# A hybrid decoder layer on one core: the output product of the convolution's rows in Strassen's blocks

## The chip, the cores and the metric

The kernel runs on one core of a Trainium2 chip. The metric is device time in microseconds for one execution. The core has a matrix engine (TensorE, "PE" in the profile, with its weight loads shown apart as "PEld"), a vector engine (VectorE, "DVE"), a scalar engine (ScalarE, "ACT"), GpSimd ("POOL") and a sync engine ("SP") that issues most transfers. A difference of 0.2% is about 1.7 us here.

## The reference, cut to what matters

```python
D_MODEL = 2048; SEQ = 512; CONV_WIDTH = ATTN_WIDTH = 1024
h = rms_norm(x, norm_g)
z = h @ w_in                       # 2048 -> 7 x 1024
...                                # causal depthwise convolution, LayerNorm, swish
y_a = (u @ conv_pw_w + conv_pw_b) * silu(a_gate)      # 512 x 1024, "the convolution's rows"
...                                # dilated window attention, 16 heads
y_b = o.reshape(bsz, s, ATTN_WIDTH) * silu(b_gate)    # 512 x 1024
y = jnp.concatenate([y_a, y_b], axis=-1) @ w_out      # (512 x 2048) @ (2048 x 2048)
return x + y
```

All inputs and the result are float32. The change concerns the last product alone: the half of its rows of `w_out` that meets `y_a`.

## The kernel before

Every tensor is held transposed: features on the 128 partitions, the 512 tokens along the free dimension. A float32 product is made of three 16-bit ones. Each operand is scaled by a power of two (from a bound on its norm, `bound`, which costs one tiny matmul over `ones16`, a reduction on VectorE and a few small operations), rounded to a high part in float16, and the rest is kept as a low part, also float16. `tri` (L360) then adds high by high, high by low, and low by high in the same PSUM bank. ScalarE makes the high part of the weights (`split_hi`, L286), VectorE the low part (`split_lo`); every VectorE call goes through one helper and so has line L72 in the profile.

The work is a list of units. A unit is 512 input features (4 tiles of 128) by 512 output features of one weight matrix, 1 MB in float32, loaded into one of six raw buffers. It takes 4 output tiles x 4 input tiles x 3 matmuls = 48 matmuls of 512 tokens. Groups of units (`GROUPS`, L48) run in a fixed order: seven input projections, the pointwise projection of the convolution (`pw`), and then the output product as `wb`, `wa` and `wc`, each for four blocks of 512 output features. `wb` meets rows 0 to 511 of `y_b` (one unit each), `wa` the 1024 rows of `y_a` (two units each), `wc` rows 512 to 1023 of `y_b` (one unit each). So the output product is 4 + 8 + 4 units.

A unit has eight slots of 6 matmuls, and `clock` counts them. The program order on each engine is written by hand: `after(n, fn)` puts a piece of work n slots later. The engines run in order, so a piece that waits holds back what is behind it on its engine. `put_y` (L551) collects `y`: part `a` from `pw`, parts `b0` and `b1` from the attention; when a part is complete its bound is taken and `split16` makes its 16-bit parts on VectorE, every second slot. `evac` (L689) adds a finished PSUM bank to `res`, which starts as `x` (`fetch_res`) and lives in four 128x512 tiles per block of output features; `wc`'s evacuation stores the row. `last_matmuls` (L760) cuts the very last output tile into 384 and 128 tokens, so that only a small evacuation and store stand behind the last matmul.

```python
def tri(ps, a, b, first, last):
    (ah, al), (bh, bl) = a, b
    T.matmul(ps, ah, bh, start=first, stop=False)
    T.matmul(ps, ah, bl, start=False, stop=False)
    T.matmul(ps, al, bh, start=False, stop=last)
```

PSUM has eight banks: four in `lin_ps` for the products, four in `s_ps` for the attention, the bounds and small sums. Four part buffers (`part_pool`) hold the float16 parts of two units.

Of the kernel before, what the change touches and what calls it, by code (L numbers as in the profile page):

```python
# [10 lines left out]
F32 = mybir.dt.float32  # L11
R32 = mybir.dt.float32r
F16 = mybir.dt.float16
# [63 lines left out]
def layer(ctx: ExitStack, tc: tile.TileContext, xt, w1, w2, w3, g_in, conv_w, conv_b,  # L77
# [34 lines left out]
    def after(n, fn):  # L112

        calendar.setdefault(clock[0] + max(n, 1), []).append(fn)
# [126 lines left out]
    for i, un in enumerate(units):  # L241
        of_group.setdefault(un[3:], []).append(i)
    n_exact = FIRST * KC // KU
    raw, parts, sums, wscale = {}, {}, {}, {}

    def load(i, cuts=(0, KU)):
# [10 lines left out]
    def measure(i):  # L257
        if n_exact <= i < len(units):
            group = units[i][3:]
            mine = of_group[group]  # L260
            j = mine.index(i)
            if j == 0:
                sums[group] = small.tile([P, len(mine)], BF16, name="wsum")
            row_squares(raw[i].rearrange("p k n -> p (k n)"), sums[group][:, j:j + 1], KU * S)
            if i == mine[-1]:
                after(4, lambda: bound("w", sums.pop(group), lambda s, v: wscale.update({group: (s, v)})))

    def exact_hi(n):

# [11 lines left out]
            after(max(6, 25 - 4 * i), lambda: measure(i + RING))  # L281

    def split_hi(i):
        if i < len(units):
            parts[i] = [part_pool.tile([P, KU, S], F16, name=n, tag="part") for n in ("wh", "wl")]
            A.activation(parts[i][0], raw[i], AF.Copy, scale=wscale[units[i][3:]][0])  # L286

    def split_lo(i):
        if i < len(units):
# [80 lines left out]
    def evac_scale(group):  # L370

        if group not in escale:
            other = {"pw": "u", "wa": "ya", "wb": "yb0", "wc": "yb1"}.get(group[0])
# [168 lines left out]

    ob, ysum = {}, {}
    yf = {"a": {}, "b0": {}, "b1": {}}
    Y_FROM = {"a": 0, "b0": 8, "b1": 12}
    y16 = {}
    WIDTH = [P * (i + 1) for i in range(NT)]
    FROM = [sum(WIDTH[:i]) for i in range(NT)]
# [1 line left out]

    def put_y(part, i, y):  # L551

        n = 8 if part == "a" else 4
        if part not in ysum:
            ysum[part] = small.tile([P, n], BF16, name=f"ysum{part}", bufs=1)
        row_squares(y, ysum[part][:, i:i + 1], S)
        yf[part][i] = y
        if len(yf[part]) == n:
            def done(s, v):
                scales["y" + part] = (s, v)  # L560
                for k in range(n):
                    after(1 + 2 * k, lambda k=k: y16.update({k + Y_FROM[part]: split16(yf[part].pop(k), s, "y16")}))
            after(2, lambda: bound(f"y{part}", ysum[part], done))

    def gate_o(i):
        if i in ob and i in bg:
# [122 lines left out]
    def evac(group, m, ps):  # L689
        kind, g = group  # L690
        i = 4 * g + m
        if kind == "vg":
            evac_vg(g, m, ps)
        elif kind == "bg":
            evac_gate(bg, group, m, ps)
            after(1, lambda: gate_o(i))
        elif kind == "ag":
            evac_gate(ag, group, m, ps)
        elif kind in "qk":
            evac_qk(g, m, ps, kind == "k")  # L700
        elif kind == "v":
            evac_v(g, m, ps)
        elif kind == "pw":
            t = temp("ya")
            V.tensor_scalar(t, ps, evac_scale(group), pwb[:, i:i + 1], op0=OP.mult, op1=OP.add)
            y = ag.pop(i)

            def gate():
                V.tensor_mul(y, y, t)
                put_y("a", i, y)  # L710

            after(1, gate)
        elif kind in ("wa", "wb"):
            V.scalar_tensor_tensor(res[i], ps, evac_scale(group), res[i], op0=OP.mult, op1=OP.add)
        else:
            t = res.pop(i)
            e = evac_scale(group)
            V.scalar_tensor_tensor(t, ps, e, t, op0=OP.mult, op1=OP.add)
            nc.sync.dma_start(out[i * P:(i + 1) * P, :], t)

    res = {}

    def fetch_res(i):
        res[i] = slot("res")
        nc.sync.dma_start(res[i], xt[i * P:(i + 1) * P, :])

    convolution = conv()
    wait = [0, False]
# [28 lines left out]
            if k == KC - 1 and a == 1:  # L757
                evac(group, m, banks.pop((group, m)))

    def last_matmuls(i, m):  # L760

        group = units[i][3:]
        t, e = res.pop(KC - 1), evac_scale(group)
        ms = slice(m * P, (m + 1) * P)
        for a, b, queue in ((0, 3 * P, nc.sync), (3 * P, S, nc.scalar)):
            ps = lin_ps.tile([P, S], F32, name="ps_l")
            for k in range(KU):
                xh, xl = y16[units[i][2] * KU + k]
                tri(ps[:, a:b], [w[:, k, ms] for w in parts[i]], (xh[:, a:b], xl[:, a:b]), k == 0, k == KU - 1)
            V.scalar_tensor_tensor(t[:, a:b], ps[:, a:b], e, t[:, a:b], op0=OP.mult, op1=OP.add)  # L770
            queue.dma_start(out[(KC - 1) * P:, a:b], t[:, a:b])

    def slot_matmuls(i, m, half_i):

        kind, g = group = units[i][3:]
        first_u, last_u = i == of_group[group][0], i == of_group[group][-1]
        if first_u and half_i == 0:
            banks[group, m] = lin_ps.tile([P, S], F32, name="ps_l")
        ps = banks[group, m]
        ms = slice(m * P, (m + 1) * P)  # L780
        wh, wl = parts[i]
        for kk in range(2):
            wk = 2 * half_i + kk
            k = units[i][2] * KU + wk
            act = (u16 if kind == "pw" else y16 if kind in OUT_K else x16)[k]
            first, last = first_u and half_i == kk == 0, last_u and half_i == kk == 1
            if kind in ("q", "k", "v"):
                tri(ps, (act[0][:, ms], act[1][:, ms]), (wh[:, wk, :], wl[:, wk, :]), first, last)
            else:
                tri(ps, (wh[:, wk, ms], wl[:, wk, ms]), act, first, last)  # L790
        if last_u and half_i == 1:
            return lambda: evac(group, m, banks.pop((group, m)))


    for i in range(4):
# [39 lines left out]
            after(8 * n_exact - 3, lambda: split_lo(n_exact))  # L835
        return todo

    for i in range(len(units)):
        kind, g = group = units[i][3:]
        exact = i < n_exact  # L840
        if exact:
            order = [(None, None)] * 8
        else:
            order = [(m, hf) for m in range(4) for hf in range(2)]
            extra = [[] for _ in range(8)]
            extra[0].append(lambda: split_hi(i + 1))
            extra[2].append(lambda: split_lo(i + 1))
            if i + 1 < len(units) and units[i + 1][3] == "wb":
                for m in range(4):
                    extra[2 * m].append(lambda m=m: fetch_res(4 * units[i + 1][4] + m))  # L850
        if kind == "pw" and i == of_group[group][0]:
            while 7 not in u16:
                next(convolution)
        for n, (m, hf) in enumerate(order):
            clock[0] = 8 * i + n
            if exact:
                extra = {n: startup(clock[0])}
            due = calendar.pop(clock[0], [])
            for fn in extra[n] + due if exact else due + extra[n]:
                fn()  # L860
            run_conv()
            if i == len(units) - 1 and m == 3:
                if hf == 0:
                    last_matmuls(i, m)
                continue
            done = exact_matmuls(clock[0]) if exact else slot_matmuls(i, m, hf)
            if done:
                done()
        if kind == "k" and i == of_group[group][-1]:
            attention(g)  # L870
    assert not calendar


# [44 lines left out]
```

## Time and profile before

| what | value |
|---|---|
| median of three runs | 840.0 us (839.9 to 840.42) |
| profiled execution, whole | 840.22 us |
| its span in the profile | 838.3 us |
| TensorE busy | 833.9 us, 99% of the span |
| VectorE busy | 610.5 us, 73% |
| ScalarE busy | 460.7 us, 55% |

The span runs from the first to the last event that the profile shows; 1.92 us of the execution lie outside it. A matmul's shown duration contains its way through the array and overlaps the next one, so the rate of TensorE is read from the distance between the starts of matmuls, not from their durations. The output product is the end of the span: `wb` from about 668.9 us, `wa` from 710.4 us, `wc` from 793.4 us to the end.

### The profile page before, as it was taken

The page shows a single profiled execution, that of the slowest core. Times are in us where ns is not written, and L with a number is a line of the kernel's source. Part 1 is how long each engine was busy: PE and PEld are TensorE (multiplying, and loading weights), DVE is VectorE, ACT ScalarE, POOL GpSimd, SP SyncE. Part 2 cuts the span into 40 slices and gives each one's busy share as a digit, 9 for nine tenths or more (in the row PEclk, how much of TensorE's full clock was granted, in tenths as well). Part 3 has the DMA queues.
Part 4 walks back from the last instruction along what each step waited for, and adds up shares of the span by engine and source line. Part 5 has one row for each costly group of instructions (what it writes and reads, how often), then busy time and mean ns, then how long its engine had stood idle before and what let it go on. Part 6 is the DMA issues. An engine that isn't in the chain of part 4 may idle for free.

```text
span 838.3 us, 11273 instructions
## 1 busy us (share of the span) xinstructions
PE 833.9 (99%) x4394; PEld 416.1 (50%) x4394; DVE 610.5 (73%) x1023; ACT 460.7 (55%) x601; POOL 90.9 (11%) x131
## 2 busy tenths in 40 slices
PE   9999999999999999999999999999999999999998
PEld 6887644444444444444444444444444444444444
DVE  6758989888888988878877869366747788344353
ACT  6676654343645449576756656576866543333110
POOL 0001010101413100004021000010000000111100
PEclk9999999999999999999999999999999999999999
DMA  9822333322343522526575625253442744221022
GB/s 338 338 100 101 105 133 108 107 100 102 102 141 108 152 94 81 140 101 170 132 176 131 156 84 158 102 139 82 126 132 101 226 168 172 100 101 51 1 101 100
DMA packets 78948, 108.15 MB, mean 129 GB/s; under 512 B 62000, under 2 KB 62384, under 8 KB 69680
## 3 DMA queue, kind: packets, MB, share of 16 engines
q1 hardware_dynamic: 78608, 107.38, 41.6%
q8 instruction: 34, 0.56, 0.3%
q14 instruction: 18, 0.15, 0.1%
q10 hardware_dynamic: 288, 0.07, 0.0%
HBM read 88.56 MB, written 4.19 MB: 111 GB/s over the span
## 4 chain that ended last, share of the span: by engine, by line
PE 99%; DMA 0%; ACT 0%; SPq 0%; DVE 0%; issue 0%; ACTq 0%
PE ps_l L362 28%; PE ps_l L364 28%; PE ps_l L363 28%; PE ps_l L755 11%; PE ps_s L595 2%; PE ps_o L638 2%; DMA x<-xt_dram 0%; PE ps_s L356 0%; PE ps_s L346 0%; PE ps_s L504 0%; ACT hh L318 0%; SPq L255 0%; DVE res L72 0%; PE ps_s L194 0%; ACTq L318 0%
## 5 line engine op out<-in xcount | busy, mean ns | idle before, releaser
L286 ACT ACTIVATE wh<-wf,ws 128x2048 f16<-128x2048 f32 x68 | 135.9, 1999 | 230.8 <-PE ps_l L363 224.8
L72 DVE SCALAR_TENSOR_TENSOR wl<-wf,ws,wh 128x2048 f16<-128x2048 f32 x68 | 159.7, 2348 | 32.7 <-ACT wh L286 32.5
L72 DVE SCALAR_TENSOR_TENSOR cv<-u,cw,cv 128x511 f32<-128x511 f32 (+14 forms) x240 | 161.0, 729 | 0.0
L362 PE MATMUL ps_l<-x,wh 128*128 128x512 f16 x384 | 145.6, 379 | 0.0
L362 PE MATMUL ps_l<-wh,x 128*128 128x512 f16 x384 | 145.6, 379 | 0.0
L364 PE MATMUL ps_l<-wh,x 128*128 128x512 f16 x384 | 145.5, 379 | 0.0
L363 PE MATMUL ps_l<-wl,x 128*128 128x512 f16 x384 | 145.5, 379 | 0.0
L364 PE MATMUL ps_l<-x,wl 128*128 128x512 f16 x384 | 145.5, 379 | 0.0
L363 PE MATMUL ps_l<-x,wh 128*128 128x512 f16 x384 | 145.5, 379 | 0.0
L182 ACT ACTIVATE junk<-wf 128x2048 bf16<-128x2048 f32 x68 | 129.2, 1899 | 4.3 <-DMA wf<-w_dram 3.9
L362 PEld LDWEIGHTS <-wh 128*128 128x128 f16 x708 | 69.3, 98 | 85.1 <-issue 3.9
L364 PEld LDWEIGHTS <-wl 128*128 128x128 f16 x708 | 69.2, 98 | 83.0
L363 PEld LDWEIGHTS <-wh 128*128 128x128 f16 x708 | 69.2, 98 | 79.3 <-issue 0.7
L363 PE MATMUL ps_l<-y,wh 128*128 128x512 f16 (+1 forms) x260 | 97.5, 376 | 0.0
L362 PE MATMUL ps_l<-y,wh 128*128 128x512 f16 (+1 forms) x260 | 97.5, 376 | 0.0
L364 PE MATMUL ps_l<-y,wl 128*128 128x512 f16 (+1 forms) x260 | 97.5, 376 | 0.0
L72 DVE SCALAR_TENSOR_TENSOR res<-ps_l,esc,res 128x512 f32<-128x512 f32 (+2 forms) x49 | 36.1, 738 | 60.3 <-PE ps_l L364 54.0
L196 POOL TENSOR_SCALAR ws<-ws 128x1 f32<-128x1 f32 x26 | 9.7, 374 | 492.3 <-DVE ws L72 492.3
L362 PEld LDWEIGHTS <-x 128*128 128x128 f16 x384 | 37.5, 98 | 46.5 <-issue 1.9
L364 PEld LDWEIGHTS <-x 128*128 128x128 f16 x384 | 37.6, 98 | 45.3
L363 PEld LDWEIGHTS <-x 128*128 128x128 f16 x384 | 37.5, 98 | 43.9
L755 PE MATMUL ps_l<-xr,wr 128*128 128x512 f32 x192 | 47.4, 395 | 0.0
(179 smaller groups left out, 880.9 us busy)
## 6 DMA issues: line engine op xcount, KB each, us to landing
wf<-w_dram SPq DMA_DIRECT2D x72, 1024.0 KB, 4.9
x<-xt_dram SPq DMA_DIRECT2D x16, 256.0 KB, 6.7
res<-xt_dram SPq DMA_DIRECT2D x16, 256.0 KB, 5.4
out_dram<-res SPq DMA_DIRECT2D x15, 256.0 KB, 2.0
wf<-w_dram SPq DMA_DIRECT2D x7, 512.0 KB, 7.2
wf<-w_dram SPq DMA_DIRECT2D x2, 256.0 KB, 3.4
tab<-table_dram SPq DMA_DIRECT2D x1, 256.0 KB, 2.7
q<-qhl SPq DMA_TRANSPOSE x16, 3.4
```

The lines of the kernel that those rows point to most:

```text
L72: return getattr(self.engine, name)(out, src, *args, **kw)
L182: A.activation(junk[:, :n], src, AF.Square, scale=scale, accum_out=acc)
L196: G.tensor_scalar(scale, scale, 1e-30, 2.0 ** (-2 * top), op0=OP.max, op1=OP.mult)
L286: A.activation(parts[i][0], raw[i], AF.Copy, scale=wscale[units[i][3:]][0])
L362: T.matmul(ps, ah, bh, start=first, stop=False)
L363: T.matmul(ps, ah, bl, start=False, stop=False)
L364: T.matmul(ps, al, bh, start=False, stop=last)
L595: T.matmul(ps[i, a], qs[hf, q][rows, p4, i * P:w], ks[hf, k][rows, p4, :w], start=n == 0, stop=n == 2)
L638: T.matmul(po[rows, i * P:(i + 1) * P], vs[hf][j // 2][:, j % 2, 2 * p4 + a, vp * DH:(vp + 1) * DH], got["t", a][:, pp * (ALL // P) + FROM ...
L755: T.matmul(banks[group, m], wt[:, a, m * P:(m + 1) * P], xk[b], start=k == 0 and a == b == 0, stop=k == KC - 1 and a == 1)
```

## The change

`wc` is gone. `wa` now has three units per block of 512 output features: the one that was `wc` (rows 512 to 1023 of `y_b`, called plain here) and the two of `y_a`. The two units of `y_a` are a matrix of 1024 by 512 features, times 1024 by 512 tokens. Both are cut in two by two blocks, and the eight block products are replaced by the seven of Strassen's method in Winograd's form, each 512 features by 256 outputs by 256 tokens: 2 x 4 x 3 = 24 matmuls of 256 tokens. Four sums of weight blocks (`s1` to `s4`) are made in place on VectorE before they are split, four sums of `y` blocks (`t1` to `t4`) likewise in `y_sums`. The plain unit is taken in 256-token blocks too (four products of 24 matmuls), since its results go to the same quarter banks. The products are put together on VectorE: some straight into `res`, `p1` through a copy by ScalarE (`alone`), `p6` and `p7` in `both`. In the last block of outputs `p6` is added in other places, and the last product is cut into two times 128 tokens. `y`'s high parts move from VectorE to ScalarE, one block each slot; `y_a` and the second part of `y_b` share one bound. `res` becomes eight 128x2x512 tiles in other pools.

A block of outputs ("group" below) is 22 steps of 12 matmuls. Numbers in the plans are steps; a negative one lies in the group before.

```diff
-GROUPS += [(kind, g) for kind in ("wb", "wa", "wc") for g in range(4)]
-OUT_K = {"wb": (2,), "wa": (0, 1), "wc": (3,)}
+GROUPS += [(kind, g) for kind in ("wb", "wa") for g in range(4)]
+OUT_K = {"wb": (2,), "wa": (3, 0, 1)}
...
+    def y_sums(k):
+        b11, b12 = (yf["a"][k][:, f:f + H] for f in (0, H))
+        b21, b22 = (yf["a"][k + 4][:, f:f + H] for f in (0, H))
...
+        V.tensor_sub(t1, b11, b12)
+        V.tensor_sub(t3, b12, b22)
+        def rest():
+            V.tensor_add(t2, b22, t1)
+            V.tensor_sub(t4, b21, t2)
+        after(1, rest)
...
+    def y_parts(s, v):
...
+            A.activation(t[:, 0], src, AF.Copy, scale=s)
+            after(1, lambda: V.scalar_tensor_tensor(t[:, 1], src, s, t[:, 0], op0=OP.mult, op1=OP.subtract))
...
+        n = 1
+        for name in ("b11", None, "t4", "t1", "t3", "b21", "t2", "b22"):
+            for k in range(4):
+                after(n, lambda name=name, k=k: block(name, k) if name else plain(k))
+                n += 1
...
+    SEVEN = 22
+    SUMS = {"s1": ("a21", "a22", "a22"), "s3": ("a11", "a21", "a21"), "s2": ("a22", "a11", "a11"), "s4": ("a11", "a12", "a12")}
...
+        def add(name):
+            x, y, to = SUMS[name]
+            V.tensor_tensor(block(to), block(x), block(y), op=OP.add)
+        def hi(name):
+            t = wparts[g, name] = part_pool.tile([P, 2, KU, H], F16, name="ws", tag="part")
+            A.activation(t[:, 0], block(name), AF.Copy, scale=wscale["wa", g][0])
+        def lo(name):
+            t = wparts[g, name]
+            V.scalar_tensor_tensor(t[:, 1], block(name), wscale["wa", g][0], t[:, 0], op0=OP.mult, op1=OP.subtract)
...
+        plan = [((-8, -12)[g > 0], plain_hi), ((-6, -11)[g > 0], plain_lo)]
+        for name, n in (("a11", -6), ("a22", -4), ("s1", -1 if g else 0), ("s3", 1), ("a12", 2), ("s2", 12), ("s4", 14)):
+            plan += [(n, lambda name=name: hi(name)), (n + 1, lambda name=name: lo(name))]
+        for name, n in (("s1", -2), ("s3", 0), ("s2", 4), ("s4", 5)):
+            plan.insert(0, (n, lambda name=name: add(name)))
...
+        LAST_3 = ((0, 0, H), (1, 0, P), (1, P, H))
+        banks_of = {"p1": (("a11", "b11"),), "v": ("22",), "z": ("12", ("s4", "b22")), "u": ("21", ("a22", "t4")),
+                    "x": ("11", ("a12", "b21")), "p5": (("s1", "t1"),), "p7": (("s3", "t3"),), "p6": (("s2", "t2"),)}
...
+        def both():
+            q = got["s"]
+            less(q, "p6", q)
+            h = temp("p67", shape=[P, 2, H])
+            V.scalar_tensor_tensor(h, ps["p7"][0], e, q, op0=OP.mult, op1=OP.add)
+            add("12", q, OP.subtract)
+            for block in ("22", "21"):
+                add(block, h)
+                store(block)
...
+        plan = [(2, alone), (4, lambda: into("22", "v")), (6, lambda: add("11", got["s"])), (12, lambda: into("21", "u")),
+                (14, lambda: into("22", "p5", ne)), (15, lambda: into("12", "p5")), (18, lambda: (into("11", "x"), store("11"))),
+                (20, both)]
+        order = (("p1", 0), ("v", 0), ("z", 0), ("u", 0), ("x", 0), ("u", 1), ("p5", 0), ("p7", 0), ("x", 1), ("p6", 0), ("z", 1))
...
+        plan += [(8, lambda: add("12", got["s"])), (16, p71), (17, lambda: add("21", got["h"])), (17, lambda: add("22", got["h"])),
+                 (20, lambda: product("z", 1, 0)), (20, lambda: into("12", "p6", ne)), (20, lambda: end(0, 0, H)),
+                 (20, lambda: (into("22", "p6"), store("22"))), (20, lambda: (into("21", "p6"), store("21"))),
+                 (21, lambda: product("z", 1, 1))]
+        last.extend([lambda: end(1, 0, P), lambda: end(1, P, H, nc.scalar)])
...
+    for g in range(4):
+        plan = seven_parts(g) + [(n + SEVEN, fn) for n, fn in seven_parts(g + 1)] + seven_products(g)
```

The rest of the diff adapts `measure`, `put_y`, `evac` and `fetch_res` to this, removes `last_matmuls`, and ends the loop over units before the first `wa`.

## Rows read from the trace of the kernel before

**Rows 1.** The page's busy times, TensorE's and its granted clock over 40 slices
```profile
PE 833.9 (99%) x4394; PEld 416.1 (50%) x4394; DVE 610.5 (73%) x1023; ACT 460.7 (55%) x601; POOL 90.9 (11%) x131
...
PEclk9999999999999999999999999999999999999999
```

**Rows 2.** The page's chain that ended last, by line
```profile
PE ps_l L362 28%; PE ps_l L364 28%; PE ps_l L363 28%; PE ps_l L755 11%; PE ps_s L595 2%; PE ps_o L638 2%; DMA x<-xt_dram 0%; PE ps_s L356 0%; PE ps_s L346 0%; PE ps_s L504 0%; ACT hh L318 0%; SPq L255 0%; DVE res L72 0%; PE ps_s L194 0%; ACTq L318 0%
```

**Rows 3.** Stretches of the output product: length, each engine's busy time (instructions), clock, DMA
```profile
668.90:710.40 41.50, 41.50 (x247) 19.61 (x246) 34.01 (x55) 17.05 (x17) 3.93 (x12) 1.00 0.49 173
710.40:793.40 83.00, 83.00 (x391) 37.70 (x390) 32.76 (x42) 27.49 (x20) 14.06 (x19) 1.00 0.20 69
793.40:834.90 41.50, 41.50 (x205) 19.43 (x203) 18.99 (x20) 6.01 (x3) 0.19 (x1) 1.00 0.25 95
```

**Rows 4.** Timeline of TensorE at the end: start, duration, operation
```profile
819.98 0.38 PE L362 MATMUL ps_l<-y,wh 128*128 128x512 f16 x1
...
832.28 0.33 PE L362 MATMUL ps_l<-y,wh 128*128 128x384 f16 x1
...
834.24 0.22 PE L362 MATMUL ps_l<-y,wh 128*128 128x128 f16 x1
...
834.85 0.22 PE L364 MATMUL ps_l<-y,wl 128*128 128x128 f16 x1
```

**Rows 5.** Groups of weight loads: count, busy us, mean ns of one
```profile
L363 PEld LDWEIGHTS <-wh 128*128 128x128 f16 x708 | 69.2, 98 | 79.3 <-issue 0.7
```

**Rows 6.** Timeline, one pair of heads' value products, merged
```profile
669.67 1.87 PE L638 MATMUL ps_o<-pt,v 128*64 128x128 f16 x60
```

**Rows 7.** Timeline of TensorE around one bound's matmul (L194)
```profile
622.67 0.38 PE L364 MATMUL ps_l<-u,wl 128*128 128x512 f16 x1
622.89 0.17 PE L194 MATMUL ps_s<-wsum,ones 128*128 128x1 bf16 x1
622.92 0.38 PE L362 MATMUL ps_l<-u,wh 128*128 128x512 f16 x1
```

**Rows 8.** VectorE's groups by shape from 655 us on
```profile
L72 DVE SCALAR_TENSOR_TENSOR wl<-wf,ws,wh 128x2048 f16<-128x2048 f32 x17 | 39.9, 2346 | 2.5 <-ACT wh L286 2.5
L72 DVE SCALAR_TENSOR_TENSOR res<-ps_l,esc,res 128x512 f32<-128x512 f32 x47 | 35.1, 749 | 59.1 <-PE ps_l L364 52.8 <-POOL esc L375 4.8 <-PE ps_s L194 1.3
...
L72 DVE TENSOR_TENSOR gate<-gate,ya 128x512 f32<-128x512 f32 x4 | 2.8, 692 | 0.1
...
L72 DVE TENSOR_SCALAR y<-gate,yas 128x512 f16<-128x512 f32 x4 | 1.9, 482 | 0.0
...
L72 DVE SCALAR_TENSOR_TENSOR hl<-sx,st,hl 128x256 f16<-128x256 f32 x1 | 0.5, 480 | 0.0
...
L72 DVE SCALAR_TENSOR_TENSOR res<-ps_l,esc,res 128x128 f32<-128x128 f32 x1 | 0.4, 351 | 0.1
```

**Rows 9.** Timeline of VectorE: the last piece of y, and two evacuations in a row
```profile
671.58 0.75 DVE L72 SCALAR_TENSOR_TENSOR gate<-ps_o,osc,gate 128x512 f32<-128x512 f32 x1 [0.83 <-PE ps_o L638]
...
703.71 1.41 DVE L72 SCALAR_TENSOR_TENSOR res<-ps_l,esc,res 128x512 f32<-128x512 f32 x2
```

**Rows 10.** ScalarE's groups by shape from 640 us on
```profile
L286 ACT ACTIVATE wh<-wf,ws 128x2048 f16<-128x2048 f32 x17 | 34.0, 2000 | 94.2 <-PE ps_l L363 94.2
L182 ACT ACTIVATE junk<-wf 128x2048 bf16<-128x2048 f32 x13 | 24.7, 1900 | 3.2 <-DMA wf<-w_dram 3.1
L182 ACT ACTIVATE junk<-gate 128x512 bf16<-128x512 f32 x5 | 3.1, 630 | 7.0 <-DVE gate L72 5.2 <-DVE ws L72 1.8
```

**Rows 11.** Timeline of TensorE: the bound of the last piece of y
```profile
676.68 0.17 PE L194 MATMUL ps_s<-ysumb,ones 128*128 128x4 bf16 x1
```

**Rows 12.** Timeline behind the last matmul: last two evacuations and both stores
```profile
834.44 1.02 DVE L72 SCALAR_TENSOR_TENSOR res<-ps_l,esc,res 128x384 f32<-128x384 f32 x2 [1.20 <-PE ps_l L364]
...
835.08 0.33 SPq L771 DMA_DIRECT2D out_dram<-res  x1
835.49 0.35 ACTq L771 DMA_DIRECT2D out_dram<-res  x1
```

More of the change, by code (lines that the diff above doesn't have):

```diff
@@ L265, in measure @@
             if i == mine[-1]:
-                after(4, lambda: bound("w", sums.pop(group), lambda s, v: wscale.update({group: (s, v)})))
+                after(4, lambda: bound("w", sums.pop(group), lambda s, v: wscale.update({group: (s, v)}),
+                                       TOP - (group[0] == "wa")))
     def exact_hi(n):
@@ L288, in split_lo @@
     def split_lo(i):
-        if i < len(units):
+        if i < n_plain:
             wh, wl = parts[i]
@@ L551, in put_y @@
     def put_y(part, i, y):
[L553 to L556, printed above, removed]
+        whole, n, at = ("b0", 4, i) if part == "b0" else ("ab", 12, i + 8 * (part == "b1"))
+        if whole not in ysum:
+            ysum[whole] = small.tile([P, n], BF16, name=f"ysum{whole}", bufs=1)
+        row_squares(y, ysum[whole][:, at:at + 1], S)
         yf[part][i] = y
-        if len(yf[part]) == n:
+        if part == "b0" and len(yf[part]) == n:
@@ new lines, in y_parts, with block, plain @@
+    def y_parts(s, v):
+        scales["yab"] = (s, v)
+        place = {}
+        def block(name, k):
+            with_ = {"b11": "t4", "t1": "b21", "t3": "t2"}.get(name)
+            if name == "b22":
+                if k % 2 == 0:
+                    place["b22", k // 2] = slots.tile([P, 2, 2, H], F16, name="y16", tag="slot")
+                t = place["b22", k // 2][:, k % 2]
+            elif with_:
+                place[with_, k] = slots.tile([P, 2, 2, H], F16, name="y16", tag="slot")
+                t = place[with_, k][:, 0]
+            else:
+                t = place[name, k][:, 1]
+            src = yt.pop((name, k))
+            tparts[name, k] = (t[:, 0], t[:, 1])
+            A.activation(t[:, 0], src, AF.Copy, scale=s)
+            after(1, lambda: V.scalar_tensor_tensor(t[:, 1], src, s, t[:, 0], op0=OP.mult, op1=OP.subtract))
+        def plain(k):
+            t = slots.tile([P, 2, S], F16, name="y16", tag="slot")
+            src = yf["b1"].pop(k)
+            y16[12 + k] = (t[:, 0], t[:, 1])
+            A.activation(t[:, 0], src, AF.Copy, scale=s)
+            after(1, lambda: V.scalar_tensor_tensor(t[:, 1], src, s, t[:, 0], op0=OP.mult, op1=OP.subtract))
+        n = 1
[3 more added lines that the diff above has]
+                n += 1
@@ L712, in evac, with fetch_res @@
             after(1, gate)
-        elif kind in ("wa", "wb"):
-            V.scalar_tensor_tensor(res[i], ps, evac_scale(group), res[i], op0=OP.mult, op1=OP.add)
-        else:
[L716 to L725, printed above, removed]
+        elif kind == "wb":
+            r = res[i // 2][:, i % 2]
+            V.scalar_tensor_tensor(r, ps, evac_scale(group), r, op0=OP.mult, op1=OP.add)
+    res = {}
+    rows_of = lambda t, j: t[2 * j * P:2 * (j + 1) * P].rearrange("(m p) t -> p m t", p=P)
+    def fetch_res(j):
+        if j < 6:
+            res[j] = wide_tile("res", [P, 2, S], F32)
+        else:
+            res[j] = att.tile([P, 2, S], F32, name="res", tag="att")
+        nc.sync.dma_start(res[j], rows_of(xt, j))
     convolution = conv()
@@ L758, in exact_matmuls @@
                 evac(group, m, banks.pop((group, m)))
[L760 to L771, printed above, removed]
     def slot_matmuls(i, m, half_i):
@@ L792, in slot_matmuls, with seven_parts, block, free @@
             return lambda: evac(group, m, banks.pop((group, m)))
+    SEVEN = 22
+    SUMS = {"s1": ("a21", "a22", "a22"), "s3": ("a11", "a21", "a21"), "s2": ("a22", "a11", "a11"), "s4": ("a11", "a12", "a12")}
+    PLACE = {"s1": "a22", "s3": "a21", "s2": "a11", "s4": "a12"}
+    wparts, plain_w, last = {}, [], []
+    def seven_parts(g):
+        if g == 4:
+            return []
+        of = of_group["wa", g]
+        def block(name):
+            name = PLACE.get(name, name)
+            return raw[of[1 if name[2] == "1" else 2]][:, :, H * (name[1] == "2"):][:, :, :H]
+        def add(name):
[7 more added lines that the diff above has]
+            V.scalar_tensor_tensor(t[:, 1], block(name), wscale["wa", g][0], t[:, 0], op0=OP.mult, op1=OP.subtract)
+            if name in ("s2", "s4"):
+                free(of[1 if name == "s2" else 2])
+        def free(i):
+            raw.pop(i)
+            if i + RING < len(units):
+                load(i + RING)
+                after(9, lambda: measure(i + RING))
+        def plain_hi():
+            if not plain_w:
+                plain_w.extend(att.tile([P, KU, S], F16, name=n, tag="att") for n in ("wh", "wl"))
+            A.activation(plain_w[0], raw[of[0]], AF.Copy, scale=wscale["wa", g][0])
+        def plain_lo():
+            V.scalar_tensor_tensor(plain_w[1], raw[of[0]], wscale["wa", g][0], plain_w[0], op0=OP.mult, op1=OP.subtract)
+            free(of[0])
+        plan = [((-8, -12)[g > 0], plain_hi), ((-6, -11)[g > 0], plain_lo)]
[3 more added lines that the diff above has]
+            plan.insert(0, (n, lambda name=name: add(name)))
+        return plan
@@ L836, in startup @@
         return todo
-    for i in range(len(units)):
+    for i in range(n_plain):
         kind, g = group = units[i][3:]
@@ L848, in layer @@
             if i + 1 < len(units) and units[i + 1][3] == "wb":
-                for m in range(4):
-                    extra[2 * m].append(lambda m=m: fetch_res(4 * units[i + 1][4] + m))
+                for m in range(2):
+                    extra[4 * m].append(lambda m=m: fetch_res(2 * units[i + 1][4] + m))
         if kind == "pw" and i == of_group[group][0]:
@@ L861, in layer @@
             run_conv()
[L862 to L865, printed above, removed]
             done = exact_matmuls(clock[0]) if exact else slot_matmuls(i, m, hf)
@@ L870, in layer @@
             attention(g)
+    for g in range(4):
+        plan = seven_parts(g) + [(n + SEVEN, fn) for n, fn in seven_parts(g + 1)] + seven_products(g)
+        for n in range(SEVEN):
+            clock[0] = 8 * n_plain + SEVEN * g + n
+            for fn in calendar.pop(clock[0], []):
+                fn()
+            for k, fn in plan:
+                if k == n:
+                    fn()
+    for fn in last:
+        fn()
     assert not calendar
```

88 lines of the change are left out of this document (82 added, 6 removed).

## The prediction

> **What bounds the kernel now.** I read the page's busy times first. The reader sees TensorE at 99% of the span with the granted clock at its full level, 2.4 GHz, in every slice [rows 1]. The chain that ended last says the same: it is matmuls from one end to the other, and 84% of it is the three lines of `tri` [rows 2]. So time is saved only by fewer or quicker matmuls, and any wait that TensorE does not have now is paid in full. Next I cut out the stage that the change touches. From 668.9 us to 834.9 us TensorE is busy without a gap, while VectorE has 34.0 of 41.5 us in `wb`, 32.8 of 83.0 us in `wa` and 19.0 of 41.5 us in `wc` [rows 3]. There is room on VectorE, but mostly late, and little in `wb`.
>
> **The rate of TensorE.** The timeline of the last unit has three widths in one stream [rows 4]. From 819.98 to 832.28 us there are 57 starts of 512 tokens: 215.8 ns each. From 832.28 to 834.24 us there are 12 of 384: 163.3 ns. From 834.24 to 834.85 us there are 11 steps of 128: 55.5 ns. No row shows 256 full-height columns. The line through 512 and 128 gives 0.417 ns a column and 108.9 ns at 256; through 384 and 128 it is 109.4 ns; half of the 512 price is 107.9 ns. I take 108.9 and keep the other two as bounds.
>
> **What the edit does to TensorE's work.** Before, `wa` and `wc` are 12 units of 48 matmuls, the last 12 of them cut in two: 564 x 215.8 + 12 x 163.3 + 12 x 55.5 ns = 121.71 + 1.96 + 0.67 = 124.34 us. (The stage from 710.4 to 834.9 us is 124.5 us [rows 3, 4]; the rest is small bound matmuls.) After, a group has 7 products of 24 for `y_a` and 4 of 24 for the plain unit, 264 matmuls of 256 tokens, four times 1056. In the last group 24 of them become 48 of 128. That is 1032 x 108.9 + 48 x 55.5 ns = 112.38 + 2.66 = 115.05 us. The difference is -9.29 us (-8.78 at 109.4 ns, -10.33 at 107.9 ns). Note how thin it is: one product in eight of `y_a` is gone, but the fixed part of each matmul (about 2 ns by the line) is now paid nearly twice as often, also in the plain unit, which saves no columns.
>
> **The weight loads.** Every matmul has its own load, 98 ns [rows 5], and there are now 1080 loads where there were 588. At 108.9 ns a matmul they would keep the load path 90% busy. Two rows say that loads do not add: 12 matmuls of 128 tokens, each with its own load, start every 55.5 ns [rows 4], and 60 value products of 128 tokens, on half the columns each, take 1.87 us, 31 ns apiece [rows 6]. The first shows loads of this very shape overlapping one another. So I cost them at nothing; were load and matmul strictly in turn, each would take 207 ns.
>
> The Trainium skill's page "TensorE: Matmul & The Clock Gate", section "Back-to-back issue gap", says that in a real stream of loads and matmuls the loads lift a 128-token matmul from about 56 to about 81 ns, which speaks against narrow matmuls. By that, as an estimate, 1080 matmuls would lose 25 ns each and the sum would be 27 us worse, near 858 us; by the rows it is 831. The trace does not agree with the page here: 55.5 ns with loads.
>
> **Bounds.** Four `wc` weight bounds go, and two bounds of `y` become one. One such matmul moves the next start by 0.034 us (622.67 to 622.92 us is 0.25 us, less 215.8 ns) [rows 7]. Five of them: -0.15 us (0 to -0.2).
>
> **VectorE in a group.** From the rows, a `scalar_tensor_tensor` grows by (2346-749)/1536 = 1.04 ns a column [rows 8]. So a low part or sum of 1024 columns, which no row shows, takes 0.749+0.533 = 1.28 us or 0.692+0.533 = 1.22 us. A group has 7 low parts (8.97), the plain one (2.35), 4 weight sums (4.90), 6 evacuations from PSUM (4.49), the addition of `p1` (0.69), `both` with two evacuations and three additions (3.57), and some 0.5 for a bound: 25.5 us against 22 x 12 x 108.9 ns = 28.75 us of TensorE. Neighbours overlap a little (two evacuations in 1.41 us instead of 1.50 [rows 9]), so 25.5 is the upper end, about 23 the lower. Cover is 3 to 5 us a group. It is not evenly spread: steps 20 to 27 hold `both`, the last evacuation, three sums and three low parts, about 13 us for 10.5 us of matmuls. Work then runs 2 to 3 us late. What is late next? Nearest is the low part of `a11`, issued at step 17 for step 22 of the next group, but by step 17 the queue has been empty again; `s4` has steps 14 to 20; all others have more. Five steps are 6.5 us, so I cost it at nothing on the path.
>
> **ScalarE in a group.** Scaling the Square's slope of (1900-630)/1536 = 0.83 ns a column, a high part of 1024 columns is about 2.00-0.85 = 1.15 us [rows 10]. Seven of them, the plain one, three squares with their accumulator reads and one copy make some 17 us of 28.75. The high parts wait for one of four part buffers; by the plan each is issued one step after the product that frees it, and the product that needs it comes five or more steps later, against 1.15 + 1.28 us of work. Nothing on the path.
>
> **The way into the first group.** Now `b1` and `y_a` are both needed at once. In `wb`, VectorE loses the twelve splits of `y` (12 x (0.48+0.75) = 14.8 us [rows 8]) and gains 18 low parts of 256 columns (0.48 each) and four of 512, about six of the small sums (0.42 each), two weight low parts and one weight sum: 8.6 + 3.0 + 2.5 + 3.8 = 17.9. So 34.0 becomes 37.1 of 41.5 us. In the first group the last ten low parts of `y` come on top: 25.5 + 4.8 - 0.75 = 29.5 us by full durations for 28.75 of TensorE, about 27 with overlap. Full, but in the plan each block of `y` is split five or more steps ahead of its product, and slack from `wb` goes in first. The last piece of `y` is gated at 671.58 us [rows 9] and its bound's matmul stands at 676.68 us [rows 11]: 5 us, of which the gate and its square take 1.6. The sums queued in between (about 5 us over eight slots, into a stretch with some 2 us of gaps) may make the gate 1 to 2 us late, which still fits. I take 0, with 0 to 5 us kept for the range.
>
> **Transfers.** Loads are the same in number; the `res` fetches are as many bytes in half the issues. DMA moves 69 and 95 GB/s in `wa` and `wc` [rows 3]. Stores now start in the first group instead of at 793 us. Nothing on the path.
>
> **The end.** Before, the last matmul starts at 834.85 us, the evacuations end at 835.46, the last store is issued at 835.49 [rows 12] and the span ends 2.8 us later. After, the first half of the last product, then two 512-wide additions of `p6`, then the two 128-wide ends stand in VectorE's order: 0.48 + 0.75 + 0.75 + 0.35 + 0.35 = 2.68 us (2.3 overlapped), from 0.16 us after the last step begins. The last step is 24 matmuls of 55.5 ns, so its last start is at 1.28 us and the queue ends at 2.5 to 2.8: 1.2 to 1.55 us after the last matmul's start, where it was 0.61. That is +0.6 to +0.95 us; two 256 KB stores just before the last may hold it a little more. I take +0.8 (0.5 to 1.5).
>
> **The sum.** 840.22 - 9.29 - 0.15 + 0.8 = 831.6 us against the profiled execution, which lies 0.2 above the median: 831.4 us. With the bounds 840.0 - 10.33 - 0.2 + 0.5 = 830.0 and 840.0 - 8.78 + 1.5 = 832.7; a wait or two of half a microsecond makes it 829.8 to 833.8.
>
> **Rivals.**
> - *TensorE waits at the start of the output blocks.* The first group's full VectorE [rows 3, 8] delivers a `y` block or a weight sum late. For it: 37.1 of 41.5, then up to 29.5 of 28.75 us. Against it: five or more steps of slack. Price 2 to 5 us: 833.5 to 836.5.
> - *VectorE becomes the bound in every group (slower).* Place: `seven_products`, low parts and sums over 256 of 512 columns with waits in order between them. It decides when a group takes over 28.75 + 8.6/4 = 30.9 us, 1.21 times my 25.5. At 1.3 times, 33.1 us, it costs 4 x 4.4 = 17 us: 849. Against it: the widths are priced by rows with the same element rate.
> - *The loads show.* If a load's end gates a narrow matmul by 25 ns, 1080 of them give +27: 858; strictly in turn, +106: 937. Against it stand [rows 4, 6]; for it only that the 128-token row is 12 long.
> - *The halved width eats the saving.* It needs 108.9 + 8.64 us / 1032 = 117.3 ns at 256 tokens, far off the line: about 840, within 0.2%.
>
> **How the numbers follow.** A change below 0.2% (1.7 us) can't be told from none. Chances: forecast 0.80, late blocks 0.09, halved width eats it 0.03, VectorE bound 0.06, loads 0.02. Faster 0.89, same 0.03, slower 0.08. The range takes the forecast and the late blocks, 829.6 to 836.5 us.
>
> **What would show it.** Right: starts of 256-token matmuls 108 to 110 ns apart without gaps, the chain still all TensorE, a group every 28.8 us, VectorE at 80 to 95% there, and some 4.2 us from the last matmul's start to the end of the span. Wrong: idle before matmuls released by VectorE or ScalarE at steps 0, 12 or 20 of a group (the late blocks, the bound), or an even pace of over 112 ns (width or loads).

## The result and the profile after

The changed kernel takes 832.76 us (median of 4 runs, 832.41 to 833.01) against 840.21 us beside it: 7.45 us less, a ratio of 0.991 (95% interval 0.9893 to 0.9927). The forecast was 831.4 us in a range of 829.6 to 836.5. The profiled execution took 832.79 us with a span of 831.0 us.

The page of the changed kernel, its busy times and the start of the chain that ended last. They answer to [rows 1, 2]; L364 to L366 are now `tri`.

```profile
PE 825.6 (99%) x4881; PEld 462.8 (56%) x4881; DVE 658.8 (79%) x1087; ACT 492.1 (59%) x657; POOL 83.4 (10%) x121
...
PE 99%; DMA 0%; DVE 0%; ACT 0%; SPq 0%; DVEq 0%; issue 0%; ACTq 0%
```

TensorE is still the bound from end to end, with 487 more matmul records and 8.3 us less busy time. The stretches of the output product (length, each engine's busy time, clock, DMA), `wb` first and then the four blocks of outputs, answer to [rows 3]:

```profile
669.60:711.10 41.50, 41.50 (x247) 19.59 (x246) 35.61 (x57) 30.17 (x44) 2.61 (x9) 1.00 0.51 184
711.10:739.90 28.80, 28.80 (x266) 25.82 (x265) 28.13 (x39) 18.61 (x23) 3.35 (x4) 1.00 0.33 116
739.90:768.80 28.90, 28.90 (x268) 25.90 (x267) 23.83 (x28) 14.26 (x15) 1.22 (x4) 1.00 0.33 115
768.80:797.60 28.80, 28.80 (x267) 25.80 (x265) 23.74 (x28) 14.16 (x13) 1.22 (x4) 1.00 0.12 38
797.60:826.50 28.90, 28.90 (x290) 26.15 (x288) 20.95 (x27) 5.09 (x6) 0.00 (x0) 1.00 0.11 37
```

The reader sees TensorE without a gap in every block, the weight loads (third number) busy 90% of the time, and VectorE (fourth) full in the first block only. The width's price is read from TensorE's timeline, from the last 512-token matmul into the first block:

```profile
710.86 0.38 PE L366 MATMUL ps_l<-y,wl 128*128 128x512 f16 x1
711.08 0.27 PE L364 MATMUL ps_l<-y,ws 128*128 128x256 f16 x1
...
721.59 0.27 PE L364 MATMUL ps_s<-y,wh 128*128 128x256 f16 x1
...
743.86 0.27 PE L364 MATMUL ps_l<-y,wh 128*128 128x256 f16 x1
```

The first and the second 256-token row are 96 starts and one bound's matmul apart: 109.5 ns with it, 109.1 without. From the first to the third there are 300 starts with one bound's matmul, 109.3 ns each. From the first such start (711.08) to the last matmul's start (826.44) the four blocks take 115.36 us.

The end, VectorE and the queues in order of time, answers to [rows 12]:

```profile
825.36 0.48 DVE L72 SCALAR_TENSOR_TENSOR res<-ps_s,esc,res 128x256 f32<-128x256 f32 x1 [0.56 <-PE ps_s L366]
825.76 1.40 DVE L72 SCALAR_TENSOR_TENSOR res<-ps_l,esc,res 128x512 f32<-128x512 f32 x2
...
826.44 0.22 PE L366 MATMUL ps_s<-y,ws 128*128 128x128 f16 x1
...
827.07 0.60 DVE L72 SCALAR_TENSOR_TENSOR res<-ps_s,esc,res 128x128 f32<-128x128 f32 x2
827.71 0.36 ACTq L944 DMA_DIRECT2D out_dram<-res  x1
```

VectorE idles 0.56 us for the first half of the last product, while two additions of `p6` that need nothing more stand behind it. They end only at 827.16, and the last evacuation at 827.67, 1.23 us after the last matmul's start, where it was 0.61. The last store is issued at 827.71 and the span ends 3.29 us later, where it was 2.81.

Term by term, in the profiled executions (before to after):

| part | forecast | measured |
|---|---|---|
| last pair's value products [rows 6] to last matmul's start | -9.44 | 165.18 to 156.07: -9.11 |
| last matmul's start to end of span | +0.8 | 3.45 to 4.56: +1.11 |
| a bound about 40 us into the span to those value products | 0 | 629.46 to 629.86: +0.40 |
| first 40 us | 0 | 40.21 to 40.51: +0.30 |
| outside the span | 0 | 1.92 to 1.79: -0.13 |
| sum | -8.64 | -7.43 |

### The profile page after: what moved, and what is told of

The parts are those of the page before. It is cut to its first block, busy times and chain, and to the rows that moved or that the text cites. A ratio compares the mean times of both kernels' runs of the same rounds, so it can differ in the third digit from the quotient of the medians.

```text
span 831.0 us, 12355 instructions
## 1 busy us (share of the span) xinstructions
PE 825.6 (99%) x4881; PEld 462.8 (56%) x4881; DVE 658.8 (79%) x1087; ACT 492.1 (59%) x657; POOL 83.4 (10%) x121
## 4 chain that ended last, share of the span: by engine, by line
PE 99%; DMA 0%; DVE 0%; ACT 0%; SPq 0%; DVEq 0%; issue 0%; ACTq 0%
PE ps_l L364 26%; PE ps_l L366 26%; PE ps_l L365 26%; PE ps_l L816 11%; PE ps_s L655 2%; PE ps_o L698 2%; PE ps_s L364 2%; PE ps_s L366 2%; PE ps_s L365 2%; DMA x<-xt_dram 0%; DVE res L72 0%; PE ps_s L358 0%; PE ps_s L348 0%; PE ps_s L506 0%; ACT hh L320 0%; SPq L256 0%
## 5 line engine op out<-in xcount | busy, mean ns | idle before, releaser
L288 ACT ACTIVATE wh<-wf,ws 128x2048 f16<-128x2048 f32 x56 | 112.0, 1999 | 143.2 <-PE ps_l L365 137.2
L72 DVE SCALAR_TENSOR_TENSOR wl<-wf,ws,wh 128x2048 f16<-128x2048 f32 x60 | 140.9, 2349 | 35.4 <-ACT wh L288 31.3
L364 PE MATMUL ps_l<-x,wh 128*128 128x512 f16 x384 | 145.6, 379 | 0.0
L364 PE MATMUL ps_l<-wh,x 128*128 128x512 f16 x384 | 145.6, 379 | 0.0
L366 PE MATMUL ps_l<-wh,x 128*128 128x512 f16 x384 | 145.5, 379 | 0.0
L366 PE MATMUL ps_l<-x,wl 128*128 128x512 f16 x384 | 145.5, 379 | 0.0
L364 PEld LDWEIGHTS <-wh 128*128 128x128 f16 x644 | 63.0, 98 | 64.1 <-issue 3.9
L366 PEld LDWEIGHTS <-wl 128*128 128x128 f16 x644 | 63.0, 98 | 61.9
L365 PEld LDWEIGHTS <-wh 128*128 128x128 f16 x644 | 63.0, 98 | 59.0 <-issue 0.7
L364 PEld LDWEIGHTS <-x 128*128 128x128 f16 x384 | 37.5, 98 | 46.5 <-issue 1.9
L366 PEld LDWEIGHTS <-x 128*128 128x128 f16 x384 | 37.5, 98 | 45.4
L865 ACT ACTIVATE ws<-wf,ws 128x1024 f16<-128x1024 f32 x28 | 32.0, 1147 | 46.6 <-DVE wf L72 20.4
L365 PE MATMUL ps_l<-y,ws 128*128 128x256 f16 x160 | 43.6, 273 | 0.0
L366 PE MATMUL ps_l<-y,ws 128*128 128x256 f16 x160 | 43.6, 273 | 0.0
L364 PE MATMUL ps_l<-y,ws 128*128 128x256 f16 x160 | 43.6, 273 | 0.0
```

Source lines behind the costliest of these rows:

```text
L72: return getattr(self.engine, name)(out, src, *args, **kw)
L865: A.activation(t[:, 0], block(name), AF.Copy, scale=wscale["wa", g][0])
```

## The experiments

The theory: the gain is TensorE's columns alone, less about 2.5 ns for each matmul that the halved width adds; loads, sums and `y`'s parts are hidden; the end gives some back. The rivals were narrow matmuls that show their loads, VectorE as the bound, and `y` blocks that come late. Where fractions of a microsecond count, a kernel is compared by its difference to the kernel before that ran beside it on the same chip, as the changed kernel's -7.45 us.

**The width alone.** The kernel before, `wa` and `wc` in halves of 256 tokens:

```diff
+            elif kind in ("wa", "wc"):
+                for h in range(2):
+                    hs = slice(h * 256, h * 256 + 256)
+                    tri(ps[:, hs], (wh[:, wk, ms], wl[:, wk, ms]), (act[0][:, hs], act[1][:, hs]),
+                        first and h == 0, last and h == 1)
```

> The kernel before, with each matmul of wa and wc cut into two of 256 tokens, nothing else changed: 564 become 1128. Theory (a 256-token matmul starts every 109.2 ns, as the trace of the changed kernel shows, and its load is hidden): each pair costs 2 x 109.2 - 215.8 = 2.6 ns more, +1.4 us, 841.6 us against 840.2. Rival (loads show on narrow matmuls, 25 ns each): 1128 x 25 ns, +28 us, 868. Rival (the width costs nothing): 840.2.

Measured: 841.99 us against 840.0, a ratio of 1.0026 (1.0016 to 1.0036). Its trace has 166.59 us from the last pair's value products to the last matmul's start instead of 165.18: +1.41 us, the theory's 1.4. The medians differ by 2.0 us; in four of the nine runs 2.6 to 3.0 us of the execution lie outside the span where the others have 1.8 to 2.0, so the trace is the better measure. Loads that show, at 868 us, are out. So Strassen's blocks start 1.4 us behind and win that back first.

**Narrower still.** The changed kernel with every 256-token matmul of the blocks cut in two of 128:

```diff
-                    tri(to, ws, [t[:, tokens] for t in ys], first and n == k == 0,
-                        last_ and n == len(banks_of[name]) - 1 and k == KU - 1)
+                    cut = range(0, tokens.stop - tokens.start, P)
+                    for c in cut:
+                        tri(to[:, c:c + P], ws, [t[:, tokens.start + c:tokens.start + c + P] for t in ys], first and n == k == c == 0,
+                            last_ and n == len(banks_of[name]) - 1 and k == KU - 1 and c == cut[-1])
```

> The changed kernel with every 256-token matmul of the output blocks cut into two of 128, each with its own load: 1032 become 2064. Theory (a 128-token matmul starts every 55.5 ns also in a long stream, the loads overlap one another): 1032 x (111.0 - 109.2 ns) = +1.9 us, 834.7. Rival (loads show once the stream is longer than 12 matmuls; 81 ns at 128 tokens): 1032 x (162 - 109.2 ns) = +54 us, 887. If the load of 98 ns is the floor of a step: 1032 x (196 - 109.2 ns) = +90 us, 922.

Measured: 835.4 us against 840.0, a ratio of 0.9945 (0.9931 to 0.9958); at -4.6 us it is 2.9 above the changed kernel, and the stretch of the last table's first row is 2.6 longer (158.65 us), where 1.9 was expected. One stretch of its trace, columns as above, and the start of a row of its matmuls:

```profile
770.00:800.00 30.00, 30.00 (x542) 30.00 (x540) 24.45 (x29) 14.26 (x13) 1.21 (x4) 1.00 0.11 38
```

```profile
779.78 0.22 PE L364 MATMUL ps_l<-y,wh 128*128 128x128 f16 x1
779.84 0.22 PE L365 MATMUL ps_l<-y,wh 128*128 128x128 f16 x1
779.90 0.22 PE L366 MATMUL ps_l<-y,wl 128*128 128x128 f16 x1
```

From 711.06 to 829.00 us there are 2112 starts, 55.8 ns each with three bounds between them, although one load lasts 98 ns here as in [rows 5] and the load path now counts as busy all the time. Loads of this shape overlap one another in a long stream too. The 0.3 ns above the 55.5 that was put in make 0.6 us on 2064 starts, most of what the expectation missed. The Trainium skill's page "Perfetto Trace Analysis", section "Identifying the Most-Contended Engine", offers the busy share of the weight loads as a measure of how near TensorE is to its limit. This case doesn't agree: the loads are busy 45% of the time with 512 columns (37.70 of 83.00 us in `wa` [rows 3]), 90% in the changed kernel and 100% here, and at each of the three TensorE has no gap and the distance of starts is that of the columns plus about 2.5 ns.

**The sums left out.**

```diff
-        V.tensor_sub(t1, b11, b12)
-        V.tensor_sub(t3, b12, b22)
...
+        t1, t2, t3, t4 = b11, b12, b22, b21
...
-        for name, n in (("s1", -2), ("s3", 0), ("s2", 4), ("s4", 5)):
-            plan.insert(0, (n, lambda name=name: add(name)))
```

> The changed kernel without the sums: the four weight sums of each block of outputs and the sums of y blocks are left out, the products take the unsummed blocks instead, everything else stays. VectorE has 19.5 + 6.8 us less to do. Theory (VectorE's work hides behind the matmuls): within 0.3 us of 832.8. Rival (the sums cost time in the first block of outputs, where VectorE is busy 28.1 of 28.8 us): 0.5 us or more below.

Measured: 832.59 us against 839.85 (ratio 0.9911, 0.9898 to 0.9925): -7.3, not measurably other than the changed kernel. In its trace VectorE is busy 23.7 us in the first block and 19.5 in the second, and TensorE has the same 28.8 and 28.9. The sums cost nothing that these runs can measure.

**`y`'s parts eight steps later.**

```diff
-        n = 1
+        n = 9
         for name in ("b11", None, "t4", "t1", "t3", "b21", "t2", "b22"):
```

> The changed kernel with all of y's split blocks eight steps later, so that nearly all low parts fall into the first block of outputs and the last is made three steps before its product. Theory (late blocks are absorbed up to the slack, and the slack is then nearly gone): VectorE gets 3.2 us more in the first block, the last low part of y is made at about step 20 for step 20: 0 to 2 us more, 832.8 to 834.8. Rival (blocks are already just in time): 5 us or more.

Measured: 832.78 us against 839.85 (0.9913, 0.99 to 0.9927): -7.1, no measurable change, the low end of what was expected. VectorE's timeline shows how near it came; the first of these lines holds the last two low parts of `y`:

```profile
735.52 0.87 DVE L72 SCALAR_TENSOR_TENSOR y<-gate,yabs,y 128x256 f16<-128x256 f32 x2
736.30 1.27 DVE L72 SCALAR_TENSOR_TENSOR ws<-wf,ws 128x1024 f16<-128x1024 f32 x1
```

They end at 736.4 us. The block starts at 710.7 us and its step 20, which needs them, 20 x 1.31 us later at 736.9. At least half a microsecond was left. In the changed kernel the same parts end at 727.0 us, 10 us before that step. The late blocks are no danger there.

**More work on VectorE.** Ten, then twenty more additions a block:

```diff
+        def extra(c):
+            d = temp("extra", shape=[P, 2, H])
+            for _ in range(c):
+                V.tensor_tensor(d, got["s"], got["s"], op=OP.add)
+        plan += [(n, lambda c=c: extra(c)) for n, c in ((8, 5), (9, 5))]
```

> The changed kernel with ten more 128x512 additions on VectorE in each block of outputs (five at step 8, five at step 9, into a spare tile), about 6 us a block. Theory (TensorE is the bound and VectorE has 5 to 7 us a block to spare in the second and third block; the first is full, but its lateness fits in the five steps of slack): 0 to 1 us more, 832.8 to 833.8. Rival (VectorE is already at its bound through waits in order): up to 4 x 6 = 24 us more.

> The same with twenty additions a block, about 12 us. Now VectorE should be the bound. Theory, from back-to-back times of 25.9, 21.6, 21.6 and 19 us in the four blocks against 28.8 of matmuls: excess 9.1 + 4.8 + 4.8 + 2.2 = 21 us, less some 5 us of slack: 14 to 20 us more, 847 to 853. If the time stays within 3 us, VectorE's spare time was larger than its busy time says.

Measured: 848.8 us with ten (1.0104, 1.009 to 1.0117) and 877.99 us with twenty (1.0452, 1.0432 to 1.0471). Both expectations failed, by 15 and 25 us. The kernel with ten shows why, in TensorE's waits (who waited for whom: us in total, times, longest) and in a stretch:

```profile
PE ps_l L366 <- DVE ws L72: 8.7, 3, 3.1
PE ps_l L364 <- ACT ws L865: 2.4, 1, 2.4
```

```profile
770.00:800.00 30.00, 27.60 (x232) 23.85 (x233) 27.91 (x35) 9.96 (x11) 1.51 (x2) 0.89 0.31 107
```

TensorE now waits three times for a low part of the weights and once for a high part. From the first to the last matmul of the blocks the trace has 131.4 us instead of 115.4. Of these 16.0 us, 11.7 are the four waits. The other 4.2 are pace: the granted clock is at its lower level, 1.2 GHz, from 770.5 to 777.4 us and from 808.1 to 811.5, each time in or just behind waits of TensorE of 2.4 to 2.8 us, and 41 starts there lie about 0.21 us apart.

My error was in the cover, the time of VectorE that hides behind TensorE: I took the blocks' busy times of 23.8 us, in which overlaps are counted once already, and subtracted the overlap again. And idle time is not all cover. First VectorE's waits in the second block of the changed kernel, where it idles 5.1 us, then the second block of the kernel with twenty, as a stretch and with VectorE's waits:

```profile
DVE wl L72 <- ACT wh L882: 1.9, 1, 1.9
DVE ws L72 <- ACT ws L865: 1.9, 2, 1.6
DVE ws L72 <- POOL ws L160: 1.1, 1, 1.1
```

```profile
753.00:794.20 41.20, 31.59 (x267) 26.74 (x265) 36.89 (x47) 13.55 (x14) 1.93 (x4) 0.88 0.26 94
DVE wl L72 <- ACT wh L882: 1.9, 1, 1.9
DVE ws L72 <- ACT ws L865: 1.6, 1, 1.6
```

With twenty additions VectorE sets the length of this block: it waits for ScalarE alone, ScalarE for VectorE alone, and TensorE waits 9.6 us for weights from both, so the lower clock is not what makes the block long. The two long waits in order for ScalarE's high parts (1.9 and 1.6 us) are still there; work queued elsewhere doesn't fill them. Five additions take 3.50 us from start to start of the next work, 0.70 each, so without its twenty the block would be 41.2 - 14.0 = 27.2 us of VectorE's work and waits against TensorE's 28.8. The cover in a middle block is 1.6 us, not 5.

Over all four blocks forty additions are 28.0 us and the time rose by 16.0, so about 12 us were absorbed. That is 3 us a block on average, but much of it lies in the last block, where VectorE idled 8.0 us and TensorE doesn't wait even with ten. The next forty cost 29.2 us, 0.73 each, so nothing more was absorbed.

**The end in another order.** First only VectorE's order at step 20, then `p6` two steps earlier, in the place of the second half of `x`:

```diff
-                 (20, lambda: product("z", 1, 0)), (20, lambda: into("12", "p6", ne)), (20, lambda: end(0, 0, H)),
+                 (20, lambda: product("z", 1, 0)), (20, lambda: into("12", "p6", ne)),
                  (20, lambda: (into("22", "p6"), store("22"))), (20, lambda: (into("21", "p6"), store("21"))),
-                 (21, lambda: product("z", 1, 1))]
+                 (20, lambda: end(0, 0, H)), (21, lambda: product("z", 1, 1))]
```

> The changed kernel with VectorE's order at step 20 of the last block of outputs changed: p6 is added to blocks 22 and 21 and these are stored before, not after, the evacuation that waits for the first half of the last product. Theory (the end grew because VectorE idles 0.56 us in front of that evacuation with the two additions queued behind it, and because their stores then go out just before the last one): last evacuation 0.3 to 0.5 us earlier, stores 0.5 us earlier, time -0.4 to -0.8 us, 832.0 to 832.4. Rival (the end is set by the bytes to store alone): within 0.2 us of 832.8.

```diff
+        if g == 3:
+            order = order[:8] + (order[9], order[8], order[10])
+            plan = [(n, fn) for n, fn in plan if n != 18]
...
-                 (20, lambda: product("z", 1, 0)), (20, lambda: into("12", "p6", ne)), (20, lambda: end(0, 0, H)),
-                 (20, lambda: (into("22", "p6"), store("22"))), (20, lambda: (into("21", "p6"), store("21"))),
+                 (18, lambda: into("12", "p6", ne)), (18, lambda: (into("22", "p6"), store("22"))),
+                 (18, lambda: (into("21", "p6"), store("21"))),
+                 (20, lambda: product("z", 1, 0)), (20, lambda: (into("11", "x"), store("11"))), (20, lambda: end(0, 0, H)),
```

> The changed kernel with p6 taken two steps earlier in the last block of outputs, in the place of the second half of x, so that only one 256 KB store and one 512-wide evacuation are left for step 20. Theory (the end grew by work of VectorE and stores behind p6): the last evacuation ends about 0.6 us behind the last matmul's start, as in the kernel before, and the last store lands about 2.8 us after its issue: -0.9 to -1.2 us, 831.6 to 831.9. Rival (bytes alone): -0.3 at most, 832.5. Rival (s2's parts are then late for p6): TensorE idles before p6 and the time rises by up to 1 us.

Measured, both against 840.0: 832.07 us (0.9906, 0.9892 to 0.9919) and 831.2 us (0.9895, 0.9881 to 0.9908). At -7.9 and -8.8 us they are 0.5 and 1.35 below the changed kernel, against 0.4 to 0.8 and 0.9 to 1.2 expected. Their intervals overlap that of the changed kernel, so the traces must show what moved. Matmuls are untouched: both traces have 156.07 us from the value products to the last start. VectorE and ScalarE's queue at the end with `p6` early:

```profile
825.65 0.35 DVE L72 SCALAR_TENSOR_TENSOR res<-ps_s,esc,res 128x128 f32<-128x128 f32 x1 [0.19 <-PE ps_s L366]
...
826.32 0.35 DVE L72 SCALAR_TENSOR_TENSOR res<-ps_s,esc,res 128x128 f32<-128x128 f32 x1 [0.32 <-PE ps_s L366]
826.70 0.35 ACTq L944 DMA_DIRECT2D out_dram<-res  x1
```

VectorE now waits for TensorE before each of the last pieces, the evacuations end 0.61 us after the last start (826.06), and the span ends at 829.4, 2.70 us behind the last store's issue. From the last start to the end of the span that is 3.34 us instead of 4.56, so 1.2 of the 1.35 us are this end, and the rest is less than the runs differ among themselves. With VectorE's order alone the evacuations end 0.61 us after the last start as well, but two 256 KB stores still go out at 826.54 and 827.08 us, beside the last one at 827.01, and the span ends 3.3 us behind that one. So VectorE's order gives back the first part of what the end had lost, and the second part comes back in the run whose stores ahead of the last one are earlier (825.49 and 826.03 us for 826.70).

**The address.** In every trace of the changed kernels so far the first stage was longer (see the last section). One more tile of 32 bytes a partition in the pool of small tiles, in the changed kernel, in the kernel before, and together with `p6` early:

```diff
+    G.memset(small.tile([P, 1], F32, name="pad", bufs=1), 0.0)
```

> The changed kernel with one more tile of 32 bytes a partition in the pool of small tiles, set once at the start by GpSimd. In the changed program that pool is 32 bytes longer than before, so the tiles of the pool behind it (xr among them) start at byte 175520 of a partition, 32 past a multiple of 64; the pad puts them on 175552. Theory (the 192 first-stage matmuls that read xr take 399 ns instead of 395 in every trace of the changed kernels because of this address, and the start is 0.3 to 0.7 us longer): xr matmuls back at 395 ns, time -0.4 to -0.7 us, 832.1 to 832.4. Rival (chance of the run): no difference, 832.8.

> The kernel before with the same 32-byte tile, which moves its xr tiles from byte 175488 to 175520. Theory (address): xr matmuls at 399 ns instead of 395, time +0.4 to +0.7 us, 840.4 to 840.7. Rival (something else in the changed program): unchanged, 840.0.

> The pad and p6 two steps earlier in the last block of outputs, together. Theory (both parts add): 831.2 less 0.4 to 0.7, 830.5 to 830.8. If only the end mattered: 831.2.

Measured, all against 840.08: 831.86 us (0.9901, 0.9886 to 0.9916), 840.47 us (1.0006, 0.9998 to 1.0015) and 830.57 us (0.9887, 0.9873 to 0.99). The medians move in the direction that the address theory says: the pad gives -0.8 us in the changed kernel (-8.2 for -7.45), a little more than the 0.4 to 0.7 expected, +0.4 in the kernel before, and -0.7 with `p6` early (-9.5 for -8.8). But the interval of the second holds no change, and those of the other two overlap the intervals of the kernels without the pad, so the traces must decide, and they do, for 0.4 us (last section). The last one is the best version: 9.5 us less than the kernel before, where the change alone gave 7.5.

## Why the prediction was right

- **TensorE's work.** Right in mechanism and nearly in size. The line through 512 and 128 tokens gave 108.9 ns; the traces show 109.1 to 109.3, inside the bounds. On 1032 matmuls that is about 0.3 us of the 0.33 that this term missed.
- **The weight loads at nothing.** Right; the 128-token experiment shows it for a stream of 2112, where the prediction had 12.
- **VectorE in a group.** Right: 23.8 us in the second and third block, forecast 23 to 25.5. The cover of 3 to 5 us is its idle time, 5.1 us there, and was too high as cover: 1.6 us are usable in a middle block. So the rival of VectorE as the bound begins 1.6 us of work a block above this kernel's, nearer than it was priced.
- **The way into the first group.** Forecast 37.1 of 41.5 us and then 27 to 29.5 of 28.75; measured 35.6 and 28.1, and no wait of TensorE.
- **ScalarE.** High parts of 1024 columns take 1.15 us, as worked out from the Square's slope. In the second block ScalarE is busy 14.3 us, where 17 was the forecast: only two of the three squares fall into that stretch.
- **The end.** The mechanism was right and the step mis-sized: "I take +0.8 (0.5 to 1.5)"; it measured +1.11, 0.62 on VectorE, at the low end of the 0.6 to 0.95 forecast, and 0.48 behind the last store's issue, with two 256 KB stores just ahead of it. The second part stood in the forecast only as a "may".
- **What was missing.** +0.40 us for the address of `xr` and +0.30 for the first 40 us were in no term. The second lies within the spread of the thirteen traces of this case, in which that start takes 39.8 to 40.7 us. Together with the end (+0.31) and the width (+0.33), less 0.13 outside the span, this is the 1.2 us between the forecast gain of 8.64 us and the 7.43 of the profiled executions.

## What to carry to other kernels

Where one stream of matmuls is the bound, price a blocking by the distance of starts at its width: here 2.5 ns for each added matmul took back a little over a tenth of what the missing product gave, and the loads nothing. Sums on another engine are free up to that engine's usable cover, which is its idle time less its waits in order (here 1.6 us of 5.1 in a middle block); find it by adding work, since busy time alone overstates it. Then look at the end: what was cut last before is no longer last, and work that needs nothing new should not stand behind an evacuation that waits.

## What the runs showed of the hardware that was not expected

The changed kernel's first stage is the same code as before, yet its float32 matmuls that read `xr` take longer. Groups of TensorE's instructions up to 98 us: the kernel before, the changed kernel, the changed kernel with the pad, and the kernel before with the pad.

```profile
L755 PE MATMUL ps_l<-xr,wr 128*128 128x512 f32 x192 | 47.4, 395 | 0.0
```

```profile
L816 PE MATMUL ps_l<-xr,wr 128*128 128x512 f32 x192 | 48.2, 399 | 0.0
```

```profile
L817 PE MATMUL ps_l<-xr,wr 128*128 128x512 f32 x192 | 47.9, 397 | 0.0
```

```profile
L756 PE MATMUL ps_l<-xr,wr 128*128 128x512 f32 x192 | 48.2, 399 | 0.0
```

The distance of starts says it more sharply: from the first bound's matmul, about 40 us into the span, to the first float16 matmul of the next stage it is 56.03 us before, 56.46 after, 56.05 after with the pad and 56.46 before with it. In the built programs `xr` starts at byte 175488, 175520, 175552 and 175520 of a partition, while the other operands of these matmuls (`hl`, `hh` and `wr`) lie at the same bytes in all four. At the two multiples of 64 the stretch takes 56.03 and 56.05 us, at 32 beyond one 0.4 us more, in either kernel. The other nine traces agree: 56.03 us with the width alone, 56.05 with the pad and `p6` early, and 56.45 to 56.46 in the seven variants of the changed kernel without the pad. It is the stretch that comes back, not each matmul: the 120 matmuls of it that read `xr` are 233.8, 238.0, 236.1 and 238.0 ns apart in the four, so the pad gives them half back, and the rest comes from the matmuls of `hl` and `hh` among them, which are quicker by 0.2 us in sum than in the changed kernel. The reason stays open. A pool of small tiles that grew by 32 bytes thus cost the change 0.4 us in a place that it didn't touch. Which of the addresses between would do the same was not tried either.
